# Low parts of the second MLP matrix: a DMA that adds the raw tile onto a negated high part, in place of a VectorE subtraction

## Chip, cores and metric

The kernel runs on one core of a Trainium2 chip. The metric is the device time of one execution in microseconds (us); lower is better.

## What is computed

Two layers of a hybrid decoder over 512 tokens of width 1024, all in float32. In each layer an input projection feeds three token mixers (a sparse attention, a gated linear attention, a causal pooling); their outputs go through an output projection, and the layer ends in an MLP:

```
h = layer_norm(DEEPNORM_ALPHA * h + mixed @ w_out[l], ln1_g[l], ln1_b[l])
ff = jnp.square(jax.nn.relu(h @ w_up[l])) @ w_down[l]
h = layer_norm(DEEPNORM_ALPHA * h + ff, ln2_g[l], ln2_b[l])
```

`w_up` is 1024 x 4096 and `w_down` is 4096 x 1024 in each layer. The change is about `w_down`, the second matrix of the MLP.

## The kernel before

**Split products.** TensorE works on a rounded 32-bit form (fp32r). To keep float32 accuracy each operand is held as two fp32r tiles, a high part `hi = round(x)` and a low part `lo = round(x - hi)`, and every product takes three matmuls (`passes`, line 516): hi by hi, hi by the matrix's lo, lo by hi. Tokens are held in four tiles of 128.

**Loading and splitting weights.** All weights go through one list of units, at most 512 KB each (`add_unit`, line 250). A unit of `w_down` is two blocks of 128 rows by 512 columns, a tile of 128 x 1024 (line 308). SyncE's queue loads the units in the order of the list into four raw buffers (`NRAW` = 4; the tile is `wr` in the profile). `splits` (line 342) takes them in the same order: ScalarE (ACT) copies the raw tile into the high part `wh` with rounding, and then VectorE (DVE) or GpSimd (POOL), whichever the planner finds free, subtracts `wh` from `wr` into the low part `wl` (`split_to`, line 350). There are four buffers for each of `wh` and `wl` (`NSPL` = 4, `room`, line 345): unit n can be split only after unit n - 4 of those that use these buffers has been read by its last matmul.

```
            act(hi, r)
            yield
            yield [free_any]
            tt(lo, r, hi, OP.subtract, "any", bias)
```

**The MLP** (`mlp`, line 1554) goes through the 4096 hidden columns in four chunks of 1024. A chunk first forms the hidden activations (`early_up` for chunk 0, `up_pairs` for chunks 1 to 3, which add and subtract quarters of pairs of `w_up` units before they are split), and then multiplies them by eight units of `w_down`: four for output columns 0 to 511 (half 0), four for columns 512 to 1023 (half 1). In the MLP's profile rows the product with `w_down` is `b<-wh,s` and `b<-wl,s` with 128x512: 24 matmuls for a unit, six for each token tile. Usually unit j is used for all four token tiles before unit j + 1. In half 1 of the last chunk the order is turned round, so that each token tile is finished early and its layer norm can begin (line 1608):

```
                    if c == 3 and hf == 1:
                        for t in range(NT):
                            yield [("bank", 1)]
                            ps = bank()
                            for j in range(4):
                                yield [("split", dn[hf][j])]
                                piece(ps, t, dn[hf][j], j)
```

There the first token tile needs all four units of the half within its 24 matmuls.

**What sets the order.** The program is written out by a planner (`Planner`, line 35) at build time. Each step is a generator; it yields a condition (an event, a free bank or buffer, an engine's estimated clock) and goes on when the planner's own estimate of time reaches it. `MM`, `act`, `tt` and `dma` add estimated costs to clocks of the engines. The order of instructions on each engine follows from these estimates; at run time each engine works through its own list in order and waits on semaphores. After `act` and `tt`, the next unit's split does not wait for the subtraction's estimated end. `loads` (line 330) asks for the split of unit i - 4 before it issues the load of unit i. `norm` (line 490) ends a layer: its two tiny POOL operations `rs` lie between VectorE operations on `h`.

Of the kernel before, what the change touches and what calls it, by code (L numbers as in the profile page):

```python
# [13 lines left out]
OP = mybir.AluOpType  # L14
# [115 lines left out]
def trunk_kernel(ctx: ExitStack, tc, x, w_in, cmp_pos, cmp_w1, cmp_w2, gla_w_gate2, gla_b_gate,  # L130
                 gla_norm_g, pool_w, pool_scale, w_out, ln1_g, ln1_b, w_up, w_down, ln2_g, ln2_b,
                 c_id, c_f32, c_bf, c_rope, out, depth=DEPTH):
    nc = tc.nc
# [9 lines left out]
    pl = Planner()  # L143
    uid = [0]

    def slot(p=128, n=512, dt=F32):
        uid[0] += 1
        pl.live += 1
        return sl.tile([p, n], dt, tag="s", name=f"s{uid[0]}")
# [18 lines left out]
    def in_psum(a):  # L168
        return a.space == PSUM

    def is_ap(a):
        return a is not None and not isinstance(a, (int, float))
# [12 lines left out]
    def act(o, a, func=AF.Copy, scale=1.0, bias=0.0, accum=None):  # L185
        n = sum(is_ap(v) for v in (scale, bias, accum))
        kw = {} if func == AF.Copy and not is_ap(bias) else {"bias": bias}
        if accum is not None:
            kw["accum_out"] = accum
        nc.scalar.activation(o, a, func, scale=scale, **kw)  # L190
        return pl.op("act", (0.051 if in_psum(a) else 0.093) + 0.833e-3 * o.free_size() + 0.093 * n,
                     [o] if accum is None else [o, accum], [a] + [v for v in (scale, bias) if is_ap(v)])

    def tt(o, a, b, op, eng="dve", bias=0.1):
        n = o.free_size()
        dve, pool = 0.065 + 1.04e-3 * n, 0.09 + 2.25e-3 * n
        if eng == "any":
            on_pool = max(pl.now, pl.clock["pool"]) + pool
            on_dve = max(pl.now, pl.clock["dve"]) + dve
            eng = "pool" if on_pool - on_dve < bias else "dve"  # L200
        e = nc.vector if eng == "dve" else nc.gpsimd
        e.tensor_tensor(out=o, in0=a, in1=b, op=op)  # L202
        return pl.op(eng, dve if eng == "dve" else pool, [o], [a, b])
# [42 lines left out]
    held = {}  # L246
    pairs = {}
    firsts = {}

    def add_unit(shape, pieces):  # L250
        units.append((shape, pieces))
        return len(units) - 1

    def cols(w, k0, nk, c0, n):
        return w.rearrange("(k p) n -> p k n", p=128)[:, k0:k0 + nk, c0:c0 + n]
# [3 lines left out]
    for l in range(depth):  # L259
        u = {}  # L260
        W = w_in[l]
        tok2 = lambda c0, n: [add_unit((2, n), [(full, cols(W, 2 * j, 2, c0, n))]) for j in range(4)]
        make = {
            "A": lambda: tok2(C_GV, 400),
            "B": lambda: [add_unit((2, 384), [
                (lambda r: r[:, :, 0:192], cols(W, 2 * j, 2, C_GQ, 192)),
                (lambda r: r[:, :, 256:384], cols(W, 2 * j, 2, C_GK, 128)),
                (lambda r: r[:, :, 192:256], cols(W, 2 * j, 2, C_GK + 128, 64))]) for j in range(4)],
            "E": lambda: [add_unit((4, 274), [
                (lambda r: r[:, :, 0:128], cols(W, 4 * j, 4, C_V1, 128)),  # L270
                (lambda r: r[:, :, 128:274], cols(W, 4 * j, 4, C_V2, 146))]) for j in range(2)],
            "D": lambda: tok2(C_K0, 384),
            "C": lambda: [add_unit((4, 256), [(full, cols(W, 4 * j, 4, C_U, 256))]) for j in range(2)],
            "F": lambda: [add_unit((8, 128), [(full, cols(W, 0, 8, C_K2, 128))])],
            "G": lambda: tok2(C_Q, 384),
            "W": lambda: [add_unit((8, 128), [
                (lambda r: r[:, :, 0:64], cols(cmp_w1[l, 0], 8 * j, 8, 0, 64)),
                (lambda r: r[:, :, 64:128], cols(cmp_w1[l, 1], 8 * j, 8, 0, 64))]) for j in range(2)],
            "O": lambda: tok2(C_OG, 384),
        }  # L280
        def early(hf):
            res, k = [], 0
            while k < len(EARLY):
                n = 2 if k + 1 < len(EARLY) and EARLY[k + 1] == EARLY[k] + 1 else 1
                res.append((add_unit((n, 512), [(full, cols(w_out[l], EARLY[k], n, 512 * hf, 512))]), EARLY[k:k + n]))
                k += n
            return res

        make["P"] = lambda: early(0)
        make["R"] = lambda: early(1)  # L290
        make["N"] = lambda: [add_unit((1, 1024), [(full, cols(w_out[l], k, 1, 0, 1024))])
                             for k in range(KT) if k not in EARLY]
        for name in ORDER:
            u[name] = make[name]()
        u["M"] = []
        for c in range(4):
            up = []
            for m in range(8):
                if c == 0 and m == NEARLY:
                    u["N2"] = make["N"]()  # L300
                if c == 0 and m < KEEP:
                    up.append([add_unit((4, 128), [(full, cols(w_up[l], 4 * j, 4, 128 * m, 128))]) for j in range(2)])
                    held.update((i, l) for i in up[-1])
                else:
                    up.append([add_unit((8, 128), [(full, cols(w_up[l], 0, 8, 1024 * c + 128 * m, 128))])])
                    if c and m % 2:
                        pairs[up[-1][0]] = up[-2][0]
            dn = [[add_unit((2, 512), [(full, cols(w_down[l], 8 * c + 2 * j, 2, 512 * hf, 512))])
                   for j in range(4)] for hf in range(2)]
            u["M"].append((up, dn))  # L310
        firsts.update({i: -1.0 for i in u["A"]} if l else {i: -99.0 for i in u["A"] + u["B"][:3]})
        plan.append(u)


    raws = {}

    def dma(o, a, size=0.0):
        nc.sync.dma_start(o, a)
        pl.clock["dma"] = max(pl.clock["dma"], pl.now) + 0.1 + size / 330e3
        pl.ready[o.tensor.name] = pl.clock["dma"] + 2.0  # L320

    def load_unit(i):
        (kk, n), pieces = units[i]
        r = wp.tile([128, kk, n], F32, tag="wraw", name=f"wr{i}", bufs=NRAW)
        for dst, src in pieces:
            dma(dst(r), src, 512.0 * kk * n / len(pieces))
        raws[i] = r
        pl.event(("raw", i), pl.ready[r.tensor.name])
# [13 lines left out]
    def splits():  # L342
        pooled, order = [], []

        def room(i):
            cond = [("used", pooled[-NSPL])] if len(pooled) >= NSPL else []
            pooled.append(i)
            return cond

        def split_to(hi, lo, r, bias):  # L350
            yield [free_act]
# [5 lines that stand above are left out]
        for i in range(len(units)):  # L357
            (kk, n), _ = units[i]
            if i in pairs:
                yield from pair_sums(pairs[i], i, room, order)  # L360
                continue
            if i in held:
                yield [("raw", i), ("h", held[i] + 0.5, 0), ("slot", 1)]
                hi, lo = [slot(dt=F32R).rearrange("p (k n) -> p k n", k=kk) for _ in range(2)]
            else:
                yield [("raw", i)] + room(i)
                hi = wp.tile([128, kk, n], F32R, tag="whi", name=f"wh{i}", bufs=NSPL)
                lo = wp.tile([128, kk, n], F32R, tag="wlo", name=f"wl{i}", bufs=NSPL)
            yield from split_to(hi, lo, raws[i], firsts.get(i, -0.2))
            parts[i] = (hi, lo)  # L370
            pl.event(("split", i))

# [61 lines left out]
    for c in FIRST:  # L434
        if c in "0123":
            t = int(c)
            dma(h[t], x[0, 128 * t:128 * t + 128, :], 524e3)
        elif c == "i":
            dma(ident, c_id, 65e3)
        else:  # L440
            load_unit(len(raws))
# [1239 lines left out]

    pl.spawn(loads(), 0)
    pl.spawn(splits(), 0)
    pl.spawn(first(), 1)
    pl.back = everything()
# [67 lines left out]
```

## Time and profile before

| | us |
|---|---|
| median of 3 runs | 1217.43 (1216.94 to 1217.57) |
| the profiled execution: its own time | 1217.37 |
| the profiled execution: span from first to last instruction | 1215.6 |
| mean granted TensorE clock | 0.994 of full speed |

The span of a profiled execution is a little shorter than its own time, which holds what lies around it. Times in the rows are microseconds from the start of the span; PE is TensorE's matmul side, PEld its weight load, DVE VectorE, ACT ScalarE, POOL GpSimd and SPq the queue of SyncE, which issues the DMAs. L177, L190, L202 and L318 are the lines of the helpers for matmuls, ScalarE operations, two-input element operations and DMA issues. Buffer numbers are left out of the tile names, so `wl<-wr,wh` is any low part of a weight tile. A matmul's row shows a time longer than the distance to the next matmul, since matmuls are pipelined.

### The profile page before, as it was taken

To read this page: it belongs to the slowest core of one execution; us is meant where nothing else is said; L and a number is where in the kernel's file an instruction comes from. 1 tells how busy PE (TensorE), PEld (TensorE's weight loads), DVE (VectorE), ACT (ScalarE), POOL (GpSimd) and SP (SyncE) were. 2 spreads that over 40 slices of the span, in tenths; PEclk is the share of its full clock that TensorE was granted. 3 is DMA by queue.
4 is the path that set the end of the run, shared out by engine and by line. 5 is a ranking of instruction groups with operands and counts; after the bars stand their busy time and mean duration, and the time that the engine had idled before them with its cause. 6 is when DMAs were issued, how large, how long until landed. Compare 5 with 4: busy or idle time off the path is not lost.

```text
span 1215.6 us, 19049 instructions
## 1 busy us (share of the span) xinstructions
PE 1192.5 (98%) x7305; PEld 1050.1 (86%) x7305; DVE 909.3 (75%) x1563; ACT 593.2 (49%) x1119; POOL 308.5 (25%) x332
## 2 busy tenths in 40 slices
PE   9999999999999999999999998999999999999997
PEld 7898788889889899899888977888998998998985
DVE  3699998886687476485667999979947864855846
ACT  4633666554337246255146445766633562552730
POOL 0255431234330010020132634303434200201202
PEclk9999999999999999999999999999999999999999
DMA  6514103143323333335144040121623233342331
GB/s 215 149 40 118 44 19 103 30 138 121 88 71 121 103 88 121 87 87 153 41 134 115 27 131 18 55 77 36 183 71 94 87 122 87 88 125 82 98 112 69
DMA packets 128523, 113.92 MB, mean 94 GB/s; under 512 B 17168, under 2 KB 103728, under 8 KB 128432
## 3 DMA queue, kind: packets, MB, share of 16 engines
q1 hardware_dynamic: 128432, 112.71, 31.1%
q8 instruction: 57, 0.93, 0.3%
q14 instruction: 34, 0.28, 0.1%
HBM read 110.59 MB, written 2.10 MB: 93 GB/s over the span
## 4 chain that ended last, share of the span: by engine, by line
PE 84%; DVE 11%; POOL 2%; ACT 1%; issue 1%; DMA 1%; POOLq 0%; SPq 0%; DVEq 0%
PE b L177 81%; DVE s L202 4%; PE b L182 3%; DVE s L215 2%; DVE nb L219 1%; POOL r L202 1%; DVE wl L202 1%; ACT s L190 1%; POOL s L202 1%; DVE h L215 0%; DMA h<-in_x_dram 0%; DVE s L208 0%; DMA wr<-in_w_up_dram 0%; DVE den L208 0%; DVE f L227 0%
## 5 line engine op out<-in xcount | busy, mean ns | idle before, releaser
L177 PE MATMUL b<-wh,s 128*128 128x512 f32 x1280 | 413.9, 397 | 0.5 <-ACT s L190 0.5
L202 DVE TENSOR_TENSOR wl<-wr,wh 128x1024 fp32r<-128x1024 f32 (+4 forms) x185 | 226.6, 1228 | 163.1 <-ACT wh L190 155.0
L190 ACT ACTIVATE wh<-wr 128x1024 fp32r<-128x1024 f32 (+4 forms) x194 | 184.4, 954 | 252.2 <-PE b L177 205.3
L177 PEld LDWEIGHTS b<-wh,s 128*128 128x128 f32 x1280 | 240.5, 188 | 54.9 <-ACT s L190 0.9
L177 PE MATMUL b<-wl,s 128*128 128x512 f32 x640 | 252.4, 394 | 0.0
L190 ACT ACTIVATE s<-s 128x512 fp32r<-128x512 f32 (+5 forms) x328 | 186.9, 587 | 99.1 <-DVE s L202 79.3
L177 PE MATMUL b<-s,s 128*128 128x256 f32 (+5 forms) x1296 | 183.7, 293 | 0.2
L190 ACT ACTIVATE s<-b 128x384 fp32r<-128x384 f32 (+8 forms) x230 | 106.5, 475 | 156.2 <-PE b L177 116.8
L177 PE MATMUL b<-hTh,wh 128*128 128x256 f32 (+1 forms) x544 | 176.0, 324 | 0.0
L177 PE MATMUL b<-hTh,wl 128*128 128x256 f32 (+1 forms) x544 | 174.6, 321 | 0.0
L177 PE MATMUL b<-hTl,wh 128*128 128x256 f32 (+1 forms) x544 | 174.4, 321 | 0.0
L177 PEld LDWEIGHTS b<-s,s 128*128 128x128 f32 (+1 forms) x1296 | 163.2, 190 | 5.2 <-DVE s L202 1.4
L202 DVE TENSOR_TENSOR s<-s,s 128x512 fp32r<-128x512 f32 (+6 forms) x190 | 145.2, 774 | 21.6 <-ACT s L190 16.0
L202 DVE TENSOR_TENSOR s<-b,s 128x256 f32<-128x256 f32 (+7 forms) x262 | 123.9, 482 | 46.4 <-PE b L177 38.1
L177 PEld LDWEIGHTS b<-wl,s 128*128 128x128 f32 x640 | 120.4, 188 | 26.5 <-POOL wl L202 0.7
L202 POOL TENSOR_TENSOR s<-wr 128x512 f32<-128x512 f32 x24 | 39.1, 1631 | 319.8 <-DMA wr<-in_w_up_dram 288.3
L177 PEld LDWEIGHTS b<-hTh,wl 128*128 128x128 f32 x544 | 102.5, 188 | 8.6
L177 PE MATMUL b<-hTh,s 128*128 128x256 f32 x576 | 109.9, 284 | 0.0
L177 PEld LDWEIGHTS b<-hTh,wh 128*128 128x128 f32 x544 | 102.5, 189 | 8.2
L177 PEld LDWEIGHTS b<-hTl,wh 128*128 128x128 f32 x544 | 102.5, 188 | 8.0
L202 POOL TENSOR_TENSOR s<-s,s 128x512 f32<-128x512 f32 (+5 forms) x54 | 72.7, 1348 | 135.7 <-DVE s L202 73.5
L177 PEld LDWEIGHTS b<-hTh,s 128*128 128x128 f32 x576 | 92.1, 191 | 0.1
(150 smaller groups left out, 1618.4 us busy)
## 6 DMA issues: line engine op xcount, KB each, us to landing
wr<-in_w_down_dram SPq DMA_DIRECT2D x64, 512.0 KB, 3.8
wr<-in_w_up_dram SPq DMA_DIRECT2D x52, 512.0 KB, 4.0
wr<-in_w_out_dram SPq DMA_DIRECT2D x20, 512.0 KB, 3.5
wr<-in_w_in_dram SPq DMA_DIRECT2D x24, 384.0 KB, 3.2
wr<-in_w_up_dram SPq DMA_DIRECT2D x24, 256.0 KB, 3.3
wr<-in_w_in_dram SPq DMA_DIRECT2D x8, 400.0 KB, 3.6
wr<-in_w_in_dram SPq DMA_DIRECT2D x6, 512.0 KB, 3.7
h<-in_x_dram SPq DMA_DIRECT2D x4, 512.0 KB, 8.4
```

Source lines behind the costliest of these rows:

```text
L177: nc.tensor.matmul(o, a, b, start=start, stop=stop, **({"skip_group_check": True} if loose else {}))
L182: nc.tensor.transpose(o, a, i)
L190: nc.scalar.activation(o, a, func, scale=scale, **kw)
L202: e.tensor_tensor(out=o, in0=a, in1=b, op=op)
L215: nc.vector.scalar_tensor_tensor(o, a, s, b, op0=op0, op1=op1)
L219: nc.vector.tensor_reduce(o, a, axis=AX.X, op=op, negate=negate)
```

## The change

The 64 units of `w_down` (eight in each of four chunks of two layers) are marked. For a marked unit ScalarE writes the high part as before and then a second time, with scale -1, into the tile of the low part. A DMA issued from GpSimd's queue then adds the raw tile onto it, so that the low part is `-hi + x`. Units that are not marked are split as before. The planner is told that such a DMA takes 1.0 us of POOL and that its result is there 3.5 us later, and the last `yield` keeps the next unit's split back, in the planner's estimate, until then.

```diff
+    added_up = set()
...
             dn = [[add_unit((2, 512), [(full, cols(w_down[l], 8 * c + 2 * j, 2, 512 * hf, 512))])
                    for j in range(4)] for hf in range(2)]
+            added_up.update(dn[0] + dn[1])
...
+    def accumulate(o, a):
+
+        nc.gpsimd.dma_start(o, a, accum_op=OP.add)
+        t = pl.op("pool", 1.0, [], [o, a])
+        pl.ready[o.tensor.name] = t + 3.5
+        pl.end = max(pl.end, t + 3.5)
...
-            yield from split_to(hi, lo, raws[i], firsts.get(i, -0.2))
+            if i in added_up:
+                yield [free_act]
+                act(hi, raws[i])
+                act(lo, raws[i], scale=-1.0)
+                yield
+                accumulate(lo, raws[i])
+                yield
+            else:
+                yield from split_to(hi, lo, raws[i], firsts.get(i, -0.2))
             parts[i] = (hi, lo)
             pl.event(("split", i))
```

## Rows read from the trace of the kernel before

**Rows 1.** The page, part 1: busy time, share of the span, instructions.
```profile
PE 1192.5 (98%) x7305; PEld 1050.1 (86%) x7305; DVE 909.3 (75%) x1563; ACT 593.2 (49%) x1119; POOL 308.5 (25%) x332
```
**Rows 2.** Chain that ended last, in order of time: start, length, what.
```profile
283.02 318.30 PE b L177 x1974
...
882.49 325.04 PE b L177 x2004
```
**Rows 3.** Busy time of each engine by stretch: length, then PE, PEld, DVE, ACT, POOL.
```profile
270.00:283.00 13.00, 12.62 (x108) 12.45 (x107) 12.90 (x17) 7.26 (x10) 7.09 (x6) 1.00 0.69 205
...
350.00:440.00 90.00, 90.00 (x558) 80.52 (x557) 59.51 (x86) 42.15 (x68) 9.21 (x6) 1.00 0.32 97
...
564.00:602.00 38.00, 38.00 (x167) 30.75 (x166) 19.54 (x28) 7.28 (x10) 3.39 (x4) 1.00 0.33 98
602.00:625.00 23.00, 21.22 (x119) 18.97 (x119) 18.90 (x27) 9.59 (x19) 10.17 (x14) 1.00 0.42 108
```
**Rows 4.** Groups of instructions by form: busy, mean ns, idle before.
```profile
L202 DVE TENSOR_TENSOR wl<-wr,wh 128x1024 fp32r<-128x1024 f32 x118 | 163.5, 1388 | 136.1 <-ACT wh L190 135.7
```
**Rows 5.** Timeline of ACT, 555 to 604 us: start, length, operation, [idle before].
```profile
574.81 1.06 ACT L190 ACTIVATE wh<-wr 128x1024 fp32r<-128x1024 f32 x1 [4.46 <-PE b L177]
580.42 1.06 ACT L190 ACTIVATE wh<-wr 128x1024 fp32r<-128x1024 f32 x1 [4.55 <-PE b L177]
586.02 1.06 ACT L190 ACTIVATE wh<-wr 128x1024 fp32r<-128x1024 f32 x1 [4.54 <-PE b L177]
601.79 0.60 ACT L190 ACTIVATE hTh<-b 128x512 fp32r<-128x512 f32 x1 [14.71 <-PE b L182]
```
**Rows 6.** Timeline of DVE, the same stretch.
```profile
575.90 1.23 DVE L202 TENSOR_TENSOR wl<-wr,wh 128x1024 fp32r<-128x1024 f32 x1 [4.30 <-ACT wh L190]
...
587.93 1.21 DVE L202 TENSOR_TENSOR wl<-wr,wh 128x1024 fp32r<-128x1024 f32 x1
```
**Rows 7.** Timeline of PE, half 1 of the last chunk, layer 0.
```profile
585.59 0.63 PE L177 MATMUL b<-wh,s 128*128 128x512 f32 x2
...
588.83 0.40 PE L177 MATMUL b<-wl,s 128*128 128x512 f32 x1
...
590.24 0.40 PE L177 MATMUL b<-wl,s 128*128 128x512 f32 x1
...
591.17 0.63 PE L177 MATMUL b<-wh,s 128*128 128x512 f32 x2
```
**Rows 8.** Timeline of ACT, 265 to 360 us: two operations back to back.
```profile
277.65 1.05 ACT L190 ACTIVATE wh<-wr 128x1024 fp32r<-128x1024 f32 x1
278.60 0.62 ACT L190 ACTIVATE s<-s 128x512 fp32r<-128x512 f32 x1
```
**Rows 9.** The page, parts 3 and 6: the queue of loads, landing times (us last).
```profile
q1 hardware_dynamic: 128432, 112.71, 31.1%
...
wr<-in_w_down_dram SPq DMA_DIRECT2D x64, 512.0 KB, 3.8
```
**Rows 10.** Issues by line, 250 to 620 us, and all loads into `wr`.
```profile
w<-in_cmp_w_dram SPq DMA_DIRECT2D x3, 16.0 KB, 2.1
```
```profile
DMA to landing us min/median/max: 2.4/3.7/9.0
```
**Rows 11.** Layer 1, the same place: timeline of ACT and of PE.
```profile
1185.23 1.06 ACT L190 ACTIVATE wh<-wr 128x1024 fp32r<-128x1024 f32 x1 [4.54 <-PE b L177]
```
```profile
1189.45 0.39 PE L177 MATMUL b<-wl,s 128*128 128x512 f32 x1
```
**Rows 12.** Busy time by stretch; the clock stands third from the end.
```profile
139.30:142.70 3.40, 1.70 (x8) 0.81 (x7) 3.23 (x6) 2.43 (x11) 3.24 (x6) 1.00 0.00 0
142.70:146.10 3.40, 2.84 (x9) 2.84 (x10) 3.19 (x11) 2.33 (x6) 1.51 (x4) 0.50 0.47 154
...
610.00:614.00 4.00, 2.39 (x15) 2.01 (x13) 3.96 (x4) 1.09 (x2) 3.27 (x5) 1.00 0.54 129
614.00:618.00 4.00, 3.83 (x23) 3.78 (x23) 3.96 (x8) 1.06 (x3) 1.67 (x2) 1.00 0.30 88
```
**Rows 13.** Chunk 0: timeline of ACT (third unit's split) and of PE (its first use).
```profile
307.35 1.06 ACT L190 ACTIVATE wh<-wr 128x1024 fp32r<-128x1024 f32 x1 [1.46 <-PE b L177]
```
```profile
321.49 0.40 PE L177 MATMUL b<-wl,s 128*128 128x512 f32 x1
```
**Rows 14.** SyncE's queue, 555 to 604 us: loads for the next layer (start, length, count).
```profile
571.63 17.90 SPq L318 DMA_DIRECT2D wr<-in_w_in_dram  x4
```

## The prediction

> **What bounds the kernel now.** I read the page's first part, then the chain that ended last, then busy time by stretch, then single timelines. The first part shows TensorE busy for 98% of the span [rows 1]; that is a mean over stages, so it does not yet say that TensorE bounds the MLP. The chain does: in layer 0 it is nothing but matmuls from 283.02 us for 318.30 us, and in layer 1 from 882.49 for 325.04 us [rows 2]. These two pieces hold nearly all of the work that the change touches. The stretches agree: between 350 and 440 us and between 564 and 602 us matmuls cover the whole length, while VectorE has 30 and 18 us to spare [rows 3]. So a subtraction on VectorE costs nothing there now, as long as its result comes before the matmul that reads it. What the change can move is that margin, and it is read where it is smallest.
>
> It is smallest in half 1 of the last chunk. ScalarE's high parts at 574.81, 580.42 and 586.02 us each wait for a matmul, because the buffer of the unit four places earlier is only then free [rows 5]. At the same moment TensorE begins half 1 with token tile 0, which wants all four units in 24 matmuls. The last matmul of half 0 starts at 585.59 us and the first of half 1 follows it in the same row. The distance between matmuls is (591.17 - 585.59) / 24 = 0.2325 us, so half 1 starts at 585.82 us. The second matmul with the fourth unit, the first that reads its low part, is number 20 and starts at 590.24 us [rows 7]. Its subtraction on VectorE starts at 587.93 and takes 1.21 us [rows 6]: ready at 589.14, 1.1 us early. Every other low part has far more; one is worked out below.
>
> **The change part by part.**
>
> *Removed.* 64 subtractions of 128x1024, at a mean of 1.39 us [rows 4], are 89 us of VectorE. In the stretches where TensorE never pauses this gains nothing. Near them TensorE is idle for 0.38 us of 270 to 283 and 1.78 us of 602 to 625 [rows 3]; I count no gain from it, since few of the removed operations lie there (bounds: 0 to 2.2 us a layer).
>
> *Added on ScalarE.* 64 negated copies. A copy of this size takes 1.06 us, and an operation behind another starts 0.95 us after it [rows 8], so 61 us in all. ScalarE is busy for 42 of 90 us between 350 and 440 us [rows 3]; eight more copies a chunk add 8 us, hidden there by the matmuls. If that cover failed, each copy would hold a PSUM evacuation back by up to 0.95 us. On the last unit the copy is in the path, and is counted below.
>
> *Added on GpSimd and the DMA engines.* 64 issues on a queue that is busy for 9 of those 90 us and 3 of the 38 [rows 3]. An issue waits for ScalarE's second copy; what stands behind it there is quarter sums, token sums and, at the layer's end, the two `rs` steps of the norm. These follow matmuls that come later than the issue, so I take zero. Each unit's raw tile is also held until the DMA has landed. The load that waits for it is four units on: at the layer's end the four of `w_in`, whose last issue now ends at 589.53 [rows 14]. It would go out near 594 and land some 4 us later, while ScalarE's next operation is at 601.79 [rows 5]; no cost.
>
> *The DMA's own time, L, from issue to landing.* The trace has no transfer inside SBUF and none that adds. Nearest is the load of 512 KB, 3.8 us; its queue moved 112.71 MB in 31.1% of the span [rows 9], so 0.524 MB takes 0.311 x 1215.6 x 0.524 / 112.71 = 1.76 us of all sixteen engines, and some 2.04 us is fixed, as the 16 KB transfers with 2.1 us also show [rows 10]. An addition must read two tiles of that size and write one. I take twice the moving part: L = 2.04 + 2 x 1.76 = 5.6 us. Ends: 2.4 us, the shortest landing of any load, and 9.0 us, the longest [rows 10].
>
> The Trainium skill, page "DMA: Bandwidth & Descriptors", section "Anatomy of one DMA", gives a DMA issued from GpSimd about 2.0 us plus its bytes over 436 GB/s, which for 512 KB is an estimate of 3.2 us. The row for the load, 3.8 us, lies above it; with 3.2 us the wait worked out next would be 1.0 us a layer, and the sum about 1219.4.
>
> *The new wait.* High part at 586.02, copy at 586.97, its end 588.03, issue 0.03 us later, the lag of VectorE's start at 575.90 behind the end of ScalarE's operation of 574.81 [rows 5, 6, 8]. So the low part is ready at 588.06 + L and wanted at 590.24: a pause of L - 2.18 us. With 5.6 us it is 3.42 us. The third unit (580.42, so 582.46 + L, wanted at 588.83 [rows 5, 7]) begins to wait at L = 6.4, but the fourth still sets the sum. Layer 1 has the same distance, 1185.23 to 1189.45 [rows 11], so 3.42 us again. Everything behind the pause (the other three token tiles, the norm, the next layer) hangs on these matmuls, so it is not made up.
>
> *The clock.* Where TensorE was busy for only 1.70 of 3.40 us its granted clock was 0.50 in the next 3.40 us, the 1.2 GHz level; after 2.39 of 4.00 us it stayed at 1.00 [rows 12]. A pause of 3.42 us is more idle than the first, so I count one such stretch at half speed in each layer: 3.4 / 2 = 1.7 us. Ends: 0 and two stretches, 3.4 us.
>
> *The other stages.* The tightest low part elsewhere is the third unit of chunk 0: high part at 307.35, so ready at 309.39 + L, wanted at 321.49 [rows 13]; it waits only from L = 12.1. No cost.
>
> **Sum.** 2 x (3.42 + 1.7) = 10.2 us on the profiled execution's own 1217.37 us: 1227.6 us. The median of the runs is 0.06 us higher, which changes nothing. With L = 3.8 and no change of clock it is 1217.4 + 2 x 1.6 = 1220.6; with L = 9.0 and one stretch, 1217.4 + 2 x 8.5 = 1234.4; with two stretches, 1237.8.
>
> **The rivals.** A measurement of this kernel can tell some 0.2%, 2.4 us, from no change.
>
> *The DMA lands almost in time.* L of 2.4 to 3.4 us gives 0.2 to 1.2 us a layer, without a change of clock: 1217.8 to 1219.8, no change. For it: loads of 2.4 us exist. Against it: the median for this size is 3.8 with one stream to read, and the adding DMA has two. By the estimate from the page cited above, 3.2 us, this case would hold. Chance 0.14.
>
> *VectorE's relief counts.* The place is the layer's turn, 270 to 283 and 602 to 625 us, where VectorE is busy for 12.9 of 13 and 18.9 of 23 us and TensorE waits for it at times; if the freed VectorE time closed every gap, it would give 2 x 2.2 us, 1213.0. It decides only if L is below 2.2, so that the new wait does not appear, and the operations removed must lie in front of the norm. Faster; chance 0.06.
>
> *The adding DMA is slow.* From L = 12.1 other stages wait too. At L = 15 the last half pauses for 12.8 us, with 1.7 for the clock, and chunk 0 for 2.9: 2 x 17.4 gives 1252. Against it: no load took over 9.0 us, and the queue's engines are busy for about a third of the time. Chance 0.10.
>
> **How the numbers follow.** The forecast, a pause at the last half alone, has 0.70. The range from 1218.5 to 1238 takes in L from 2.7 to about 10.7; left out are the relief (0.06), half of the almost-in-time case (0.06) and the larger part of the slow DMA (0.08). Faster 0.06, same 0.14, slower 0.70 + 0.10 = 0.80.
>
> **What would show it.** Of the changed kernel's profile: no `wl` subtraction of 128x1024 left on VectorE in the `w_down` stages; ScalarE with two copies a unit; a GpSimd DMA with a landing time, to be set against 5.6 us. TensorE should have one pause, after 18 or 19 matmuls of half 1 of the last chunk in each layer, released by a DMA, with a half-speed stretch right after, and none elsewhere in the MLP. It would be wrong if the low parts land within 2.2 us, if pauses appear in the first three chunks, or if TensorE waits for ScalarE or GpSimd instead.

## The result, and the profile after

| | before | after |
|---|---|---|
| median, us | 1217.5 (4 runs) | 1265.01 (4 runs, 1263.47 to 1267.49) |
| ratio, 95% interval | | 1.039 [1.0367, 1.0413] |
| profiled execution: own time, us | 1217.37 | 1267.49 |
| its span, us | 1215.6 | 1265.7 |
| its mean granted clock | 0.994 | 0.993 |

The change makes the kernel 47.5 us slower. The forecast was slower by 10.2 us, with a range that ended at 1238. The direction is right, the time is far outside.

The page of the kernel after, parts 1, 5 and 6:

```profile
PE 1202.2 (95%) x7305; PEld 1052.8 (83%) x7305; DVE 846.3 (67%) x1499; ACT 648.8 (51%) x1183; POOL 353.4 (28%) x396
...
L326 POOL DMA_DIRECT2D wl<-wr x64 | 55.9, 873 | 265.1 <-ACT wl L190 224.9
...
wr<-in_w_down_dram SPq DMA_DIRECT2D x64, 512.0 KB, 4.7
wl<-wr POOLq DMA_DIRECT2D x64, 512.0 KB, 5.7
```

Against [rows 1] VectorE has lost 63 us and 64 instructions, ScalarE has gained 64 instructions and 56 us, GpSimd 64 issues of 0.87 us. The forecast had 89 us for VectorE. The subtractions of this form did fall from 163.5 us (118) to 71.7 us (54), but other operations of VectorE take longer now, `s<-wr,wr` for instance 1041 ns in the mean and not 681; why was not tried. The kernel does what the change says. The adding DMA lands after a median of 5.7 us; the forecast took 5.6. So the price of the new operation was close, and most of the loss must be sought elsewhere.

It is found by cutting the trace at the stages. In each layer there are four products with `w_down` (192 matmuls each: `b<-wh,s` and `b<-wl,s` with 128x512) and between them the three pairs of `w_up` for the next chunk. From the first start and the last end of each such block, in us:

| | before | after | added in all |
|---|---|---|---|
| the stretches between `w_down` products, layer 0 | 39.63, 39.80, 39.67 | 48.07, 46.10, 46.03 | 21.1 |
| the same, layer 1 | 39.69, 39.59, 39.80 | 45.90, 46.23, 46.39 | 19.4 |
| the last `w_down` product, layers 0 and 1 | 46.09, 44.80 | 51.42, 49.58 | 10.1 |
| the six other `w_down` products together | 268.36 | 268.50 | 0.1 |

These sum to 50.7 us; the two spans differ by 50.1. (The profiled execution of the kernel after took 1267.49 us, 2.5 above the median of its runs, so these sums lie above the 47.5.) The last product costs what was forecast (10.2). The other 40.5 us lie in six stretches in which no matmul reads a low part that the change makes; of the change only the copies and DMAs for the first units of the next product run there.

What TensorE waits for there. Waits of the kernel before and then of the kernel after, by engine and what ended them: total us, times, longest.

```profile
ACT s L190 <- DVE s L202: 79.3, 54, 3.3
...
DVE h L202 <- PE b L177: 10.3, 11, 2.5
...
PE b L177 <- DVE wl L202: 1.8, 1, 1.8
```

```profile
ACT s L190 <- DVE s L202: 182.0, 60, 12.8
DVE h L202 <- PE b L177: 157.2, 28, 15.3
...
PE b L177 <- DVE wl L202: 28.9, 19, 2.0
PE b L177 <- DMA wl<-wr: 6.1, 4, 2.6
```

TensorE now waits for VectorE, although VectorE has less to do than before; its four waits for a DMA, 6.1 us, all lie in the two last products. The four pauses of the first stretch, from the timeline of PE, kernel after, 362 to 402 us (start, length, operation, [idle before]):

```profile
364.86 1.46 PE L177 MATMUL b<-s,s 128*128 128x256 f32 x10 [0.88 <-DVE s L202]
...
372.20 0.38 PE L177 MATMUL b<-s,wl 128*128 128x256 f32 x1 [1.35 <-DVE wl L202]
...
384.47 0.39 PE L177 MATMUL b<-s,wl 128*128 128x256 f32 x1 [2.00 <-DVE wl L202]
...
399.13 0.39 PE L177 MATMUL b<-hTh,wl 128*128 128x256 f32 x1 [1.49 <-DVE wl L202]
```

The busy time by stretch around them, kernel after (length, then PE, PEld, DVE, ACT, POOL; the clock stands third from the end), shows the clock at its full level through the second pause and behind it, and lower after the third, the longest:

```profile
370.00:373.00 3.00, 1.65 (x14) 1.44 (x13) 3.00 (x5) 2.72 (x5) 1.06 (x1) 1.00 0.14 42
373.00:376.00 3.00, 3.00 (x28) 3.00 (x27) 2.99 (x5) 0.88 (x2) 0.30 (x1) 1.00 0.09 19
...
383.00:386.40 3.40, 1.93 (x12) 1.93 (x13) 3.31 (x7) 2.46 (x5) 0.00 (x0) 0.85 0.00 0
386.40:390.00 3.60, 3.60 (x23) 3.60 (x23) 2.14 (x4) 1.12 (x3) 0.00 (x0) 0.67 0.65 186
```

A pause is counted from the end shown for the matmul before it. Such a matmul shows 0.28 us, but twelve of them start between 395.82 and 397.13 us, 0.12 us apart, and the first one after the last pause takes 0.23 us to the next; so each pause costs some 0.16 + 0.11 = 0.27 us more than its row says. The four are 0.88 + 1.35 + 2.00 + 1.49 = 5.7 us; with 4 x 0.27 = 1.1 and, for the clock, 3.4 x 0.15 + 3.6 x 0.33 = 1.7 us they make 8.5, against 48.07 - 39.63 = 8.4 found. In the other five stretches there are the same four pauses, 5.2 to 5.7 us in all, and the clock stays at 1.00; with the 1.1 us they make 6.3 to 6.8, against 6.2 to 6.6 found.

Why VectorE is late stands in its own list. VectorE's timeline, kernel after, around the end of the first `w_down` product (`h<-h,b` adds the product to `h`, here that of half 1; `s<-s,wr` and the like are the quarter sums of the first `w_up` pair):

```profile
340.67 2.60 DVE L202 TENSOR_TENSOR wl<-wr,wh 128x1024 fp32r<-128x1024 f32 x1 [2.15 <-ACT wh L190]
349.63 0.69 DVE L215 SCALAR_TENSOR_TENSOR h<-h,b 128x512 f32<-128x512 f32 x1 [6.36 <-PE b L177]
350.24 0.68 DVE L202 TENSOR_TENSOR s<-s,wr 128x512 f32<-128x512 f32 x1
351.03 0.69 DVE L215 SCALAR_TENSOR_TENSOR h<-h,b 128x512 f32<-128x512 f32 x1
351.64 1.20 DVE L202 TENSOR_TENSOR s<-wr,wr 128x512 f32<-128x512 f32 x1
```

And the kernel before, the same place:

```profile
341.14 0.68 DVE L202 TENSOR_TENSOR s<-s,wr 128x512 f32<-128x512 f32 x1
341.74 0.68 DVE L202 TENSOR_TENSOR s<-wr,wr 128x512 f32<-128x512 f32 x1
...
351.67 0.68 DVE L215 SCALAR_TENSOR_TENSOR h<-h,b 128x512 f32<-128x512 f32 x1
```

Before, these two sums of the pair are done nine microseconds ahead of the first `h` addition of half 1. After, the first of them stands behind it. VectorE then idles for 6.36 us before a matmul lets it add, with the sums queued up behind, and does everything at once when the product has ended. ScalarE's next step waits for the first of them (ACT's timeline, same kernel):

```profile
350.96 0.63 ACT L190 ACTIVATE s<-s 128x512 fp32r<-128x512 f32 x1 [10.32 <-DVE s L202]
```

So there are two theories. *Order:* what the planner books for a marked unit (two copies, 1.0 and 3.5 us) moves other instructions within the lists of VectorE and ScalarE; the lists, and not the operations, make the six stretches longer. *Operations:* the copies, issues and DMAs themselves disturb these stretches, by crowding ScalarE, by late loads or by transfers in each other's way, and the changed order costs nothing. The expectations below call them theory A and theory B.

### The profile page after: what moved, and what is told of

Its sections match the earlier page's. It is cut to its first block, busy times and chain, and to the rows that moved or that the text cites. A ratio compares the mean times of both kernels' runs of the same rounds, so it can differ in the third digit from the quotient of the medians.

```text
span 1265.7 us, 19193 instructions
## 1 busy us (share of the span) xinstructions
PE 1202.2 (95%) x7305; PEld 1052.8 (83%) x7305; DVE 846.3 (67%) x1499; ACT 648.8 (51%) x1183; POOL 353.4 (28%) x396
## 4 chain that ended last, share of the span: by engine, by line
PE 74%; DVE 16%; issue 4%; DMA 3%; POOL 2%; ACT 1%; SPq 0%; POOLq 0%; ACTq 0%; DVEq 0%
PE b L177 72%; DVE s L202 7%; PE b L182 2%; DVE wl L202 2%; DVE s L215 2%; DMA wl<-wr 1%; DVE nb L219 1%; POOL r L202 1%; POOL s L202 1%; DVE h L215 1%; DMA h<-in_x_dram 1%; ACT wh L190 1%; ACT s L190 0%; DMA wr<-in_w_up_dram 0%; DMA wr<-in_w_down_dram 0%
## 5 line engine op out<-in xcount | busy, mean ns | idle before, releaser
L202 DVE TENSOR_TENSOR wl<-wr,wh 128x1024 fp32r<-128x1024 f32 (+4 forms) x121 | 136.0, 1129 | 59.2 <-ACT wh L190 58.4
L177 PEld LDWEIGHTS b<-s,s 128*128 128x128 f32 (+1 forms) x1296 | 163.5, 191 | 11.7 <-DVE s L202 8.0
L202 DVE TENSOR_TENSOR s<-s,s 128x512 fp32r<-128x512 f32 (+6 forms) x186 | 142.3, 772 | 27.3 <-ACT s L190 22.1
L202 DVE TENSOR_TENSOR h<-h,b 128x512 f32<-128x512 f32 x64 | 43.8, 684 | 157.7 <-PE b L177 157.2
L326 POOL DMA_DIRECT2D wl<-wr x64 | 55.9, 873 | 265.1 <-ACT wl L190 224.9
L177 PEld LDWEIGHTS b<-hTh,wl 128*128 128x128 f32 x544 | 103.1, 190 | 18.6 <-DVE wl L202 10.1
L202 POOL TENSOR_TENSOR s<-s,s 128x512 f32<-128x512 f32 (+5 forms) x58 | 79.4, 1371 | 120.3 <-DVE s L202 56.2
```

The costliest lines, as they stand in the source:

```text
L177: nc.tensor.matmul(o, a, b, start=start, stop=stop, **({"skip_group_check": True} if loose else {}))
L326: nc.gpsimd.dma_start(o, a, accum_op=OP.add)
```

## Experiments

Diffs are against the kernel after unless said otherwise. Runs 1 to 4 share one chip, where the kernel before had 1216.78 us (13 runs), and 5 to 7 another, 1216.83 (15 runs).

**1. The order of before, with the DMA.** The copy and the DMA are issued, but the planner is told exactly what it was told of the subtraction. Every engine's list is then that of before, with a copy added behind each high part and a DMA of GpSimd's in the place of the subtraction. The traces bear this out: set beside that of before, the list of VectorE lacks 64 subtractions, that of ScalarE has 64 copies more and that of GpSimd 64 DMAs more; by operation and tile nothing else is changed or moved, and the lists of TensorE and SyncE are the same.

```diff
-                act(lo, raws[i], scale=-1.0)
-                yield
-                accumulate(lo, raws[i])
+                nc.scalar.activation(lo, raws[i], AF.Copy, scale=-1.0)
                 yield
+                yield [free_any]
...
+                nc.gpsimd.dma_start(lo, raws[i], accum_op=OP.add)
+                pl.op(eng, dve if eng == "dve" else pool, [lo], [raws[i], hi])
```

> The changed kernel's copies and adding DMAs, but booked in the planner as the old subtraction, so that every engine's list of instructions stands in the order of the kernel before, with 64 copies more on ScalarE, 64 DMAs more on GpSimd and 64 subtractions fewer on VectorE. Theory A (most of the loss is the order: the planner's serial booking puts the quarter sums and splits of the next w_up pairs behind the h additions on VectorE, and only the pause at the last half is the DMA's own): 1227 us, 1224 to 1231, with no pause of TensorE between the w_down stages. Theory B (the operations themselves cost it: the landing, the raw tiles held longer, ScalarE's copies, the traffic): 1250 to 1265 us, with pauses between the w_down stages as in the changed kernel.

Measured: 1227.45 us (1225.89 to 1229.0, 4 runs), 1.0091 [1.0076, 1.0106]. The six stretches are those of before to the hundredth (39.63, 39.80, 39.67; 39.69, 39.59, 39.80); the last products are 52.91 and 48.99. All of the added time is there (6.8 and 4.2 us). The chain of this kernel, last half of each layer (start, length, what):

```profile
584.86 1.06 ACT wh L190
585.92 0.96 ACT wl L381
586.88 0.28 issue
587.17 6.74 DMA wl<-wr
...
593.95 12.10 PE b L177 x43
```
```profile
1193.39 4.42 DMA wl<-wr
...
1197.86 8.31 PE b L177 x28
```

This is the path that the forecast described: high part, copy, issue, landing, matmul. The pauses are 4.72 and 2.40 us. The clock behind them (busy time by stretch, same kernel):

```profile
594.00:597.40 3.40, 3.40 (x8) 2.72 (x9) 0.88 (x2) 0.00 (x0) 0.00 (x0) 0.50 0.41 120
...
1197.90:1201.30 3.40, 3.40 (x10) 2.69 (x11) 1.55 (x3) 0.00 (x0) 0.00 (x0) 0.62 0.00 0
1201.30:1205.00 3.70, 3.70 (x16) 2.99 (x15) 2.87 (x5) 0.00 (x0) 1.71 (x2) 0.88 0.03 12
```

In layer 0 it is the 1.2 GHz level for 3.40 us, 1.7 us lost; in layer 1 the loss is 3.4 x 0.38 + 3.7 x 0.12 = 1.7 us as well.

One wait of this kernel shows that a waiting VectorE is not the harm by itself:

```profile
DVE h L202 <- PE b L177: 106.5, 24, 13.3
```

Its `h` additions wait ten times as long as before, as VectorE has less to do, and TensorE doesn't pause in the stretches, because the sums that it needs next stand in front of them, as before.

**2. The order of after, with subtractions.** The planner books two copies, 1.0 and 3.5 us as in the change; issued are the high part's copy and VectorE's subtraction. Set beside the trace of the kernel after, the lists differ by the 64 subtractions, copies and DMAs alone.

```diff
+    def subtract_late(o, a, b):
+        nc.vector.tensor_tensor(out=o, in0=a, in1=b, op=OP.subtract)
+        t = pl.op("pool", 1.0, [], [o, a])
+        pl.ready[o.tensor.name] = t + 3.5
+        pl.end = max(pl.end, t + 3.5)
...
-                act(lo, raws[i], scale=-1.0)
+                pl.op("act", 0.093 + 0.833e-3 * lo.free_size(), [lo], [raws[i]])
                 yield
-                accumulate(lo, raws[i])
+                subtract_late(lo, raws[i], hi)
```

> The opposite corner: the order of the changed kernel on every engine, but VectorE subtracts as before; no copy, no DMA. Theory A: the six stretches between w_down stages keep their 6 to 8 us each, the last half has no pause: 1255 us, 1249 to 1259. Theory B: 1217 to 1222 us.

Measured: 1258.61 us (1256.88 to 1261.05, 4 runs), 1.0348 [1.0333, 1.0364]. There is no adding DMA and no second copy in this kernel, and yet the six stretches are 46.01, 46.10, 46.01 and 46.12, 46.17, 46.16 us, with the same four pauses in each. One detail of the expectation was missed: the last half has a pause of 1.0 us in each layer, for a `wl` of VectorE. Its waits:

```profile
ACT s L190 <- DVE s L202: 200.0, 65, 12.8
...
PE b L177 <- DVE wl L202: 28.3, 19, 1.8
```

Together, the first two are a square: order alone +41.8 us, operations alone +10.7, both +47.5. The order makes the six stretches longer; the theory that the operations do falls. The sum of the two, 52.5, is 5.0 more than both together, so they share some time; the last half is one place, where this kernel already waits for late low parts (last products 47.24 and 46.09 against 46.09 and 44.80). In the profiled executions, by their spans, it is 40.7 + 10.4 = 51.1 against 50.1: the last halves share 3.3 us, and the six stretches are 2.1 us longer in the kernel after than here, 1.7 of which is the low clock in the first.

**3. As 1, but the last half by subtraction.** Half 1 of the last chunk is not marked; 56 of 64 units stay with the DMA.

```diff
-            added_up.update(dn[0] + dn[1])
+            added_up.update(dn[0] + dn[1] if c < 3 else dn[0])
```

> As the first of these four, with the eight units of half 1 of the last chunks (four in each layer) subtracted by VectorE again. Theory A with the pause at the last half as the DMA's only cost: 1217.5 us, 1216 to 1220. If other waits on the DMA or on ScalarE count: 1222 or more. Theory B: 1240 or more.

Measured: 1217.66 us (1216.37 to 1219.24, 10 runs), 1.0008 [0.9998, 1.0017]. Stretches and last products are those of before (46.09 and 44.80). So 56 copies, 56 issues and 56 DMAs, with the raw tiles held longer, cost nothing that can be measured, and the eight units of the two last halves were all the price of the operations.

Which of the bookings moves the order? A unit is booked as two copies of 0.95 us (the formula stands in the diff of 2), 1.0 and 3.5 us, and the last `yield` holds the next split back until then: 6.4 us a unit, one after the other (this is what is called the hold below). TensorE uses up a unit in 24 x 0.2325 = 5.6 us; the planner itself books 512 / 2400 + 0.0025 us for such a matmul, 5.2 us a unit. By these bookings the eight splits of a chunk fall behind TensorE in the plan, and what follows them with them.

**4. Without the hold.**

```diff
                 accumulate(lo, raws[i])
-                yield
```

> The changed kernel without the last yield behind the adding DMA, so that in the planner the next unit's split no longer waits for the landing; the 1.0 us of POOL and the 3.5 us to the landing are still booked. If the hold alone moved the order: 1227 us, 1223 to 1233. If the booked costs move it as well: 1240 to 1265. Theory B: 1250 to 1265.

Measured: 1250.72 us (1248.56 to 1252.73, 4 runs), 1.0282 [1.0266, 1.0297]. A miss for the simple form of the theory, by which the hold was all. The time alone can't tell the other two, whose ranges overlap here; theory B has fallen with experiment 2. The stretches are 43.97 to 44.15, still 4.2 to 4.5 us too long, now with one long pause each, for another engine. ScalarE's timeline of this kernel, first stretch:

```profile
389.80 1.05 ACT L190 ACTIVATE wh<-wr 128x1024 fp32r<-128x1024 f32 x1
390.74 1.05 ACT L190 ACTIVATE wl<-wr 128x1024 fp32r<-128x1024 f32 x1
391.69 0.61 ACT L190 ACTIVATE wh<-s 128x512 fp32r<-128x512 f32 x1
```

and its timeline of PE:

```profile
392.36 0.50 PE L177 MATMUL b<-s,wh 128*128 128x256 f32 x2 [2.11 <-ACT wh L190]
```

ACT's timeline of the kernel before has the last pair's `wh<-s` ahead of the copy of the `w_down` unit:

```profile
384.82 0.64 ACT L190 ACTIVATE wh<-s 128x512 fp32r<-128x512 f32 x1
...
389.45 1.05 ACT L190 ACTIVATE wh<-wr 128x1024 fp32r<-128x1024 f32 x1
```

So without the hold the early `w_down` units go too far forward, and two copies of one of them stand in front of what TensorE needs first. After the pause the clock is at its lower level once more (busy time by stretch, same kernel):

```profile
394.00:397.40 3.40, 3.40 (x18) 3.40 (x17) 0.42 (x1) 0.14 (x1) 0.00 (x0) 0.50 0.97 252
```

**5. Without the hold, and the second copy issued but not booked.**

```diff
-                act(lo, raws[i], scale=-1.0)
+                nc.scalar.activation(lo, raws[i], AF.Copy, scale=-1.0)
                 yield
                 accumulate(lo, raws[i])
-                yield
```

> The run without the hold, and the second copy on ScalarE issued but not booked in the planner. The run without the hold lost 4.4 us in each of the six stretches between w_down stages to one pause, released by a high-part copy on ScalarE that stood behind two booked pairs of copies. If the booked copy put it there, and not the work of the copy: 1227 us, 1224 to 1232, no such pause. If the copy's own time on ScalarE did it: 1245 to 1253.

Measured: 1233.02 us (1232.32 to 1234.85, 4 runs), 1.0135 [1.012, 1.0151]. This lies 1 us above the range of the first case and 12 below that of the second. The stretches are 40.77 to 40.95, 1.1 to 1.2 us each above before; the pause for a `wh` of ScalarE is gone, and one of 0.65 to 0.71 us for a `wl` of VectorE stands in its place. The copy's booking was most of what was left in 4: the same copy runs in both, and only its place in the plan differs. The 5.6 us above experiment 1 go with what is still booked otherwise there, 1.0 us of GpSimd and 3.5 us to the landing; the two were not tried apart.

**6. With the hold, but the landing booked as 0.12 us.**

```diff
-        pl.ready[o.tensor.name] = t + 3.5
-        pl.end = max(pl.end, t + 3.5)
+        pl.ready[o.tensor.name] = t + 0.12
+        pl.end = max(pl.end, t + 0.12)
```

> The changed kernel with the hold, but the landing booked as 0.12 us behind the 1.0 us of POOL in place of 3.5 us. If the 3.5 us, held for every unit, put the quarter sums behind the h additions: the four pauses in each stretch between w_down stages go, and what is left is at most the order of the run without the hold, 1227 to 1252 us. If the hold does it at any length: 1260 to 1266 us.

Measured: 1247.33 us (1246.29 to 1248.1, 4 runs), 1.0251 [1.0237, 1.0265]. A unit is now booked as 3.0 us, less than TensorE's 5.6 or 5.2. VectorE's timeline of this kernel has the pair's sums where they were before:

```profile
342.79 0.69 DVE L202 TENSOR_TENSOR s<-s,wr 128x512 f32<-128x512 f32 x1
343.40 0.69 DVE L202 TENSOR_TENSOR s<-wr,wr 128x512 f32<-128x512 f32 x1
...
351.36 0.68 DVE L215 SCALAR_TENSOR_TENSOR h<-h,b 128x512 f32<-128x512 f32 x1
```

The four pauses are gone, and with them 2.4 to 4.6 us of each stretch (42.02 to 43.58 now; in the three longest the clock falls after the pause, in the others it doesn't). What stays is one pause of 1.65 to 1.71 us for a `wh` of ScalarE, as in 4. So the 3.5 us under the hold put the sums behind the `h` additions. That the rest is the booked copies, a second harm that comes up once the first is gone, is taken over from 4 and 5; with the hold it was not tried.

**7. The DMA in one of VectorE's fullest stretches.** Against 1: the marked units are not those of `w_down` but five a layer early on, the two units of `w_in` for the causal pooling (`C`) and the first three for the gated linear attention's output gate (`O`).

```diff
-            added_up.update(dn[0] + dn[1])
...
+        added_up.update(u["C"] + u["O"][:3])
```

> Order of the kernel before; w_down subtracted by VectorE as before; the adding DMA (with the unbooked copy) used for five other units in each layer, two of the input projection for the pooling and three for the output gate, which are split 10 to 17 us ahead of their first use while VectorE bounds the chain. If VectorE's 5.3 us of subtractions a layer there count: 1208 to 1215 us. If they stand beside other waits (POOL, ScalarE): 1216 to 1218. If the DMA or the copies are late there: 1219 or more.

Measured: 1216.36 us (1215.44 to 1217.83, 11 runs), 0.9998 [0.9989, 1.0007]. Busy time by stretch of this kernel, and then of the kernel before:

```profile
100.00:125.00 25.00, 25.00 (x112) 20.03 (x111) 19.23 (x40) 13.24 (x18) 13.22 (x12) 1.00 0.82 198
```
```profile
100.00:125.00 25.00, 25.00 (x111) 20.16 (x112) 24.28 (x45) 8.98 (x13) 10.08 (x7) 1.00 0.44 127
```

VectorE falls from 24.28 to 19.23 of 25 us, TensorE is busy throughout in both, and nothing comes of it. The expectation's words that VectorE bounds the chain there hold only for its end: up to 124 us the chain that ended last is TensorE's (24.17 us from 99.95). Behind it stands a `wl` of VectorE before, and ScalarE with the second copy here (0.83 us at 123.52), so there ScalarE's work has come in the place of VectorE's. No version here beats the kernel before.

## Why the prediction was wrong, and what of it was right

*What bounds the kernel* and *Removed*: right. VectorE was relieved of 63 us and nothing was gained by it; experiment 3 shows it for 56 units together with everything that was added, and experiment 7 in a stretch where VectorE was nearly full.

*The DMA's own time*: right in its middle. 5.6 us stood in the sum; the median of 64 is 5.7, and 6.3 in experiment 1. That an addition takes twice the moving part of a load was not tried, so the close agreement may be luck. The kernel after's DMAs into `wl`, from the view of that tile:

```profile
DMA to landing us min/median/max: 4.5/5.7/9.9
```

Even the shortest is above the 3.2 us estimated from the Trainium skill ("DMA: Bandwidth & Descriptors", "Anatomy of one DMA"). That rule held the rival in which the DMA lands almost in time; the measurement decides, and the rival fell.

*The new wait* and *The clock*: right in place and near in size. In the kernel after, layer 0, the chain has `issue` 0.28 us, where the forecast had 0.03, and a landing of 5.60:

```profile
608.03 0.28 issue
608.32 5.60 DMA wl<-wr
```

TensorE pauses for 0.77 and 2.60 us, 3.37 together, where 3.42 was forecast (in layer 1 it is one pause of 2.52 us, behind a landing of 4.49), and then has one stretch near the lower clock level (busy time by stretch, kernel after):

```profile
614.00:617.40 3.40, 3.40 (x8) 2.69 (x9) 0.94 (x2) 0.00 (x0) 0.00 (x0) 0.51 0.46 124
```

That the pause falls in two in layer 0 was missed: the third unit waited too, because its high part came only 4.27 us before the fourth's here (601.75 and 606.02 us) and not 5.60 as in [rows 5]. Experiment 1, the same edit with no other order, measured 1227.45 us where the forecast said 1227.6. This is partly luck of the two layers: landings of 6.74 and 4.42 us average to the 5.6 that was taken for both. The clock's 1.7 us a layer was no certain term either: it was lost in both layers here and in the kernel after, but in experiment 4, layer 1, a pause of 2.42 us at the same place left the clock at 1.00.

*Added on ScalarE* and *Added on GpSimd*: the operations as such cost nothing, as said (experiment 3).

*The other stages. ... No cost*: this step failed, and it is the whole of the error. It asked only whether each low part lands before its matmul, and that was so: the six other `w_down` products are unchanged, and half 0 of the last product waits once, for 0.22 us (kernel after, layer 1). It never costed the change's last lines, which alter what the planner is told. The working treated every list of instructions as that of before with some operations exchanged. The change section's own words had the term: 1.0 and 3.5 us and a `yield` that holds the next split back. With the two copies that is 6.4 us a unit in the plan against TensorE's 5.6, and from [rows 7] the 5.6 was at hand. The runs showed in its place six stretches between the `w_down` products that are 6.2 to 8.4 us longer each, 40.5 us in all, and 41.8 us from the bookings alone (experiment 2). The right question was what a planner does when eight units in a row take longer than the matmuls that eat them: it writes later work behind instructions that wait for TensorE. Each engine takes its list in order, so VectorE cannot use its free time for a sum that stands behind an `h` addition. The Trainium skill says the same of three engines ("PSUM — Partial Sum Buffer", "Engine vs sequencer instructions": the queues of ScalarE, VectorE and GpSimd are strictly first in, first out), and the traces agree: VectorE idle for 6.36 us with the sums right behind.

The range failed with this step. Its upper end came from the longest landing of a load and two stretches at the lower clock; none of the rivals had a changed order of other work, so 47 us lay outside all of them. Of the signs of failure listed under *What would show it* one came true, pauses in the first three chunks (they lie in chunks 1, 2 and 3); that TensorE would wait for VectorE, the engine relieved, was not even on the list.

What stays open: why the planner, with the hold gone, still puts the copies of the early `w_down` units ahead of the last pair's high part is only argued from its bookings (4 against 5); the step of the plan at which it decides was not followed. Of the 0.2 to 0.3 us of a pause that its row doesn't show only the sum was compared.

## What to carry to other kernels

Where a program writes out the order of the instructions by estimated costs, a change of an estimate is a change of the kernel: read what is booked for the new operation, add it up along its chain, and set it against the time in which the consumer uses up one unit. An experiment that keeps the old bookings with the new operations, and one with the new bookings and the old operations, separate the two causes in two runs. An operation moved off an engine with time to spare gained nothing here, and a DMA in its place is safe only where its landing, not its issue, is well ahead of the first reader.

## What the runs showed of the hardware

- An adding DMA of 512 KB inside SBUF lands 4.42 us (experiment 1, layer 1) and 4.49 us (kernel after, at 1233.08 us) after its issue when no load runs beside it, and 6.74 us (experiment 1, layer 0) and 5.60 us (kernel after, layer 0) beside four `w_in` loads. That the loads are the cause is read from these rows, and was not tried by itself.
- From the end of ScalarE's copy to the DMA's start 0.28 us pass, where VectorE followed ScalarE within 0.03 us; the issue holds GpSimd for 0.87 us.
- With the adding DMAs beside them the loads of `w_down` land after 4.7 us (kernel after) and 4.6 (experiment 3) instead of 3.8 [rows 9]; experiment 3 has the time of before, so it costs nothing there.
- The length of a pause of TensorE does not settle by itself whether its clock falls. After one of 2.00 us (kernel after, 384.47 us) the granted clock read 0.85 and 0.67, and after one of 2.11 us 0.50 (experiment 4). Yet after 1.99 us in the kernel after it stayed at 1.00, as the rows below show, and after 2.42 us in experiment 4 (1224.40 us) too; and of the six pauses of 1.65 to 1.71 us in experiment 6 three were followed by a lower clock and three were not.

```profile
1191.95 0.39 PE L177 MATMUL b<-s,wl 128*128 128x256 f32 x1 [1.99 <-DVE wl L202]
```
```profile
1190.40:1193.80 3.40, 1.85 (x15) 1.85 (x16) 3.40 (x7) 2.54 (x5) 0.00 (x0) 1.00 0.00 0
1193.80:1197.20 3.40, 3.40 (x31) 3.40 (x30) 3.03 (x6) 2.40 (x4) 0.00 (x0) 1.00 0.67 195
```
